# Layer norm without affine parameters: rings of 8-row tiles, statistics combined on GpSimd, a last store in two DMAs

## The chip, the cores and the metric

The kernel runs on one core of a Trainium2 chip. The metric is the device time of one execution in microseconds. Nine runs of the kernel before gave a median of 321.31 us, from 321.01 to 321.41 us. One more execution was recorded by the profiler; all instruction times below are from that one.

## The reference

For each of the 32 x 512 = 16,384 rows of 1024 float32 values the mean and the variance over the row are taken, and the row is normalised with them:

```python
mean = np.mean(x, axis=-1, keepdims=True)
var = np.var(x, axis=-1, keepdims=True)
return ((x - mean) / np.sqrt(var + eps)).astype(np.float32)   # x: (32, 512, 1024), eps = 1e-5
```

67.11 MB are read from HBM and 67.11 MB are written.

## The kernel before

The 16,384 rows are cut into 32 tiles. A tile holds K = 4 rows in each of the 128 partitions, so it is 2 MiB; a partition's four rows lie next to one another in HBM and make one run of 16 KiB. One "row" below always means one row in each of the 128 partitions, 512 KiB in all. So the input has 128 such rows.

For each tile, in the order of the code:

- SyncE (SP) issues the load into `xt` (line 47). The pool `xin` has 6 buffers, 24 rows, so load 7 has to wait until the first tile has been used.
- VectorE (DVE) takes statistics. A `bn_stats` (line 53) covers half a row, 512 values, and leaves six numbers: count, mean and sum of squared deviations, for the even and for the odd values. A `bn_aggr` for each row (line 57) combines the two halves into mean and variance. Then three small instructions on all four rows: the negated mean (line 59), variance plus eps (line 61) and its reciprocal (line 65).
- ScalarE (ACT) takes the square root, which gives `rstd` (line 68), and GpSimd (POOL) multiplies it with the negated mean (line 71).
- ACT normalises row by row (line 75): `Identity` with `scale=rstd` and `bias=nmr`, 128 x 1024 values in each instruction, into `yt`. The pool `yout` has 6 buffers, 24 rows.
- ACT issues the store (line 84).

The order of instructions on each engine is the one that the Tile framework's scheduler chose: the square root of a tile is often put among the normalising instructions of an earlier tile. Loads go through SP's hardware DMA queue (q1 in the profile), stores through ACT's (q10). Both run on the same 16 DMA engines, 8 partitions of a tile on each.

Of the kernel before, what the change touches and what calls it, by code (L numbers as in the profile page):

```python
# [1 line left out]

# [4 lines left out]


@with_exitstack  # L10
def kernel(
    ctx: ExitStack,
    tc: tile.TileContext,
    x: bass.AP,
    eps: bass.AP,
    out: bass.AP,
):
    nc = tc.nc
    P = nc.NUM_PARTITIONS

    eps_val = float(eps) if not isinstance(eps, bass.AP) else 1e-5

    x2 = x.flatten_outer_dims()
    o2 = out.flatten_outer_dims()
    N, D = x2.shape
    BN_MAX = nc.vector.BN_STATS_FMAX
    assert D % BN_MAX == 0
    NSUB = D // BN_MAX

    K = 4  # L30
    rows_per_tile = P * K
    assert N % rows_per_tile == 0
    ntiles = N // rows_per_tile

    xin = ctx.enter_context(tc.tile_pool(name="xin", bufs=6))
    yout = ctx.enter_context(tc.tile_pool(name="yout", bufs=6))
    st = ctx.enter_context(tc.tile_pool(name="st", bufs=4))

    fdt = mybir.dt.float32
    AF = mybir.ActivationFunctionType  # L40
    ALU = mybir.AluOpType

    for t in range(ntiles):
        rows = slice(t * rows_per_tile, (t + 1) * rows_per_tile)

        xt = xin.tile([P, K, D], fdt)
        nc.sync.dma_start(out=xt, in_=x2[rows].rearrange("(p k) d -> p k d", p=P))  # L47

        stats = st.tile([P, K, NSUB, 6], fdt)
        mv = st.tile([P, K, 2], fdt)  # L50
        for k in range(K):
            for s in range(NSUB):
                nc.vector.bn_stats(  # L53
                    out=stats[:, k, s, :],
                    in_=xt[:, k, s * BN_MAX : (s + 1) * BN_MAX],
                )
            nc.vector.bn_aggr(out=mv[:, k, :], in_=stats[:, k, :, :])  # L57
        negmean = st.tile([P, K], fdt)
        nc.vector.tensor_scalar_mul(out=negmean, in0=mv[:, :, 0], scalar1=-1.0)  # L59
        vpe = st.tile([P, K], fdt)  # L60
        nc.vector.tensor_scalar(  # L61
            out=vpe, in0=mv[:, :, 1], scalar1=eps_val, scalar2=None, op0=ALU.add
        )
        ivar = st.tile([P, K], fdt)
        nc.vector.reciprocal(out=ivar, in_=vpe)  # L65

        rstd = st.tile([P, K], fdt)
        nc.scalar.activation(out=rstd, in_=ivar, func=AF.Sqrt, bias=0.0, scale=1.0)  # L68

        nmr = st.tile([P, K], fdt)  # L70
        nc.gpsimd.tensor_mul(out=nmr, in0=negmean, in1=rstd)  # L71

        yt = yout.tile([P, K, D], fdt)
        for k in range(K):
            nc.scalar.activation(  # L75
                out=yt[:, k, :],
                in_=xt[:, k, :],
                func=AF.Identity,
                bias=nmr[:, k : k + 1],
                scale=rstd[:, k : k + 1],  # L80
            )

        dst = o2[rows].rearrange("(p k) d -> p k d", p=P)
        nc.scalar.dma_start(out=dst, in_=yt)  # L84


# [1 line left out]
_INS = ['x', 'eps']  # L88
_OUTS = [((32, 512, 1024), 'float32')]
#: Inputs that are plain numbers.  # L90
_NUMBERS = {'eps': 1e-05}


# [26 lines left out]
```

## Time and profile before

| | us |
|---|---|
| median of nine runs | 321.31 |
| the profiled execution | 320.97 |
| its span, first to last instruction | 318.9 |
| VectorE busy | 181.7 |
| ScalarE busy | 154.2 |
| GpSimd busy | 6.6 |
| normalising, one row (line 75), mean | 1.227 |
| `bn_stats`, half a row (line 53), mean | 0.665 |
| `bn_aggr` (line 57), mean | 0.196 |
| small product on GpSimd (line 71), mean | 0.201 |

The span leaves out 2.07 us of the profiled execution, and that execution is 0.34 us under the median. An instruction's own duration can overlap with the next one's on its engine: in the timeline two `bn_stats` in a row last 1.23 us together, and four normalising instructions 4.63 us. The page adds for the transfers that the 16 DMA engines moved 134.27 MB in the span, and that 6 packets with 0.05 MB came from a queue of kind "instruction": the engines' programs are fetched by the same DMA engines.

### The profile page before, as it was taken

What the parts mean: (1) busy time and instruction counts of PE and PEld (TensorE: products, weight loads), DVE (VectorE), ACT (ScalarE), POOL (GpSimd) and SP (SyncE); (2) the same over time, 40 slices, a digit from 0 to 9 for tenths busy, and PEclk for the clock granted to TensorE, in tenths of its full rate; (3) what the DMA queues carried; (4) which work ended last, traced back from release to release, by engine and by line L of the source; (5) the groups of instructions that cost most, each with busy time, mean ns of one, the idle gap of its engine ahead of it and who ended that gap; (6) DMA issues with size and microseconds to landing.
All of it is one profiled execution on the core that took longest, in us unless ns stands there. A gap on an engine that the chain in (4) does not pass through costs nothing.

```text
span 318.9 us, 926 instructions
## 1 busy us (share of the span) xinstructions
DVE 181.7 (57%) x480; ACT 154.2 (48%) x161; POOL 6.6 (2%) x36
## 2 busy tenths in 40 slices
DVE  0999764457754377544676355765446744467610
ACT  1147491651907419074380833809247091470970
POOL 0000000000000000000000000000000000000000
DMA  7999999999999999999999999999999999999995
GB/s 294 430 411 420 438 434 430 427 429 429 428 434 433 434 430 429 430 430 430 432 438 434 431 430 427 430 430 432 434 434 433 426 432 430 430 427 427 425 427 218
DMA packets 9222, 134.27 MB, mean 421 GB/s; under 512 B 1024, under 2 KB 1024, under 8 KB 1024
## 3 DMA queue, kind: packets, MB, share of 16 engines
q1 hardware_dynamic: 4608, 67.11, 49.6%
q10 hardware_dynamic: 4608, 67.11, 49.2%
q14 instruction: 6, 0.05, 0.0%
HBM read 67.11 MB, written 67.11 MB: 421 GB/s over the span
## 4 chain that ended last, share of the span: by engine, by line
DMA 84%; ACT 4%; issue 4%; DVE 4%; SPq 1%; POOLq 0%; POOL 0%; ACTq 0%; DVEq 0%
DMA xt<-in_x_dram 84%; ACT yt L75 4%; DVE stats L53 3%; SPq L47 1%; DVE mv L57 0%; ACT rstd L68 0%; DVE ivar L65 0%; DVE negmean L59 0%; POOLq L115 0%; POOL nmr L71 0%; DVE vpe L61 0%; ACTq L84 0%; DVEq L65 0%; DVEq L59 0%; ACTq L75 0%
## 5 line engine op out<-in xcount | busy, mean ns | idle before, releaser
L53 DVE BATCH_NORM_STATS2 stats<-xt 128x6 f32<-128x512 f32 x256 | 159.4, 665 | 115.1 <-DMA xt<-in_x_dram 115.1
L75 ACT ACTIVATE yt<-xt,nmr,rstd 128x1024 f32<-128x1024 f32 x128 | 146.7, 1227 | 4.7 <-POOL nmr L71 4.5
L68 ACT ACTIVATE rstd<-ivar 128x4 f32<-128x4 f32 x32 | 6.5, 204 | 149.5 <-DVE ivar L65 149.0
L57 DVE BATCH_NORM_AGGREGATE mv<-stats 128x2 f32<-128x12 f32 x128 | 25.1, 196 | 1.1
L71 POOL TENSOR_TENSOR nmr<-negmean,rstd 128x4 f32<-128x4 f32 x32 | 6.4, 201 | 297.7 <-ACT rstd L68 297.7
L65 DVE RECIPROCAL ivar<-vpe 128x4 f32<-128x4 f32 x32 | 5.7, 178 | 3.0
L59 DVE TENSOR_SCALAR negmean<-mv 128x4 f32<-128x4 f32 x32 | 5.5, 170 | 3.1
L61 DVE TENSOR_SCALAR vpe<-mv 128x4 f32<-128x4 f32 x32 | 5.2, 162 | 0.0
L68 ACT ACT_TABLE_LOAD x1 | 1.3, 1283 | 0.7 <-PEq L101 0.7
L101 POOL MEMSET const-float32-0.0<- 128x1 f32 x1 | 0.1, 99 | 0.2 <-issue 0.2
L101 POOL MEMSET const-bfloat16-1.0<- 128x1 bf16 x1 | 0.1, 102 | 0.0
L101 POOL MEMSET const-uint8-127<- 128x1 uint8 x1 | 0.1, 102 | 0.0
L101 POOL MEMSET const-float32-1.0<- 128x1 f32 x1 | 0.1, 99 | 0.0
## 6 DMA issues: line engine op xcount, KB each, us to landing
xt<-in_x_dram SPq DMA_DIRECT2D x32, 2048.0 KB, 38.4
out_dram<-yt ACTq DMA_DIRECT2D x32, 2048.0 KB, 15.4
```

The lines of the kernel that those rows point to most:

```text
L47: nc.sync.dma_start(out=xt, in_=x2[rows].rearrange("(p k) d -> p k d", p=P))
L53: nc.vector.bn_stats(out=stats[:, k, s, :], in_=xt[:, k, s * BN_MAX : (s + 1) * BN_MAX],)
L57: nc.vector.bn_aggr(out=mv[:, k, :], in_=stats[:, k, :, :])
L59: nc.vector.tensor_scalar_mul(out=negmean, in0=mv[:, :, 0], scalar1=-1.0)
L61: nc.vector.tensor_scalar(out=vpe, in0=mv[:, :, 1], scalar1=eps_val, scalar2=None, op0=ALU.add)
L65: nc.vector.reciprocal(out=ivar, in_=vpe)
L68: nc.scalar.activation(out=rstd, in_=ivar, func=AF.Sqrt, bias=0.0, scale=1.0)
L71: nc.gpsimd.tensor_mul(out=nmr, in0=negmean, in1=rstd)
L75: nc.scalar.activation(out=yt[:, k, :], in_=xt[:, k, :], func=AF.Identity, bias=nmr[:, k : k + 1], scale=rstd[:, k : k + 1],)
L101: nc = _bacc.Bacc("TRN2", target_bir_lowering=False, num_devices=1)
```

## The change

Tiles are 8 rows high (4 MiB, 32 KiB in each partition), 15 of them, and then tiles of 4, 2 and 2 rows. Instead of two pools there are two fixed buffers, used as rings: `xr` for 32 rows of x, and `yr` for 16 rows of y. The framework's scheduler is off (`manual_schedule`): each engine executes in the order of the code.

`bn_aggr` and the small VectorE instructions after it are gone. GpSimd combines the four partial means and four sums of squared deviations of all 8 rows of a tile with nine instructions (the lines of `pool_sum` and `group`), ACT takes the square root of the variance plus eps, VectorE the reciprocal, and GpSimd the product with the negated mean. `std`'s square root now comes before the reciprocal, so VectorE's reciprocal waits for ACT. VectorE goes on to the next tile's `bn_stats` only after it.

The store of the last tile is issued as two DMAs, one for partitions 0 to 119 and one for partitions 120 to 127.

```diff
+TILES = (8, 8, 8, 8, 8, 8, 8, 8, 8, 8, 8, 8, 8, 8, 8, 4, 2, 2)
+XRING = 32
+YRING = 16
+GROUP = 8
+
+def place(tiles, ring):
+    plan, row, pos = [], 0, 0
+    for K in tiles:
+        if pos + K > ring:
+            pos = 0
+        plan.append((K, row, pos))
+        row += K
+        pos += K
+    return plan
...
-    xin = ctx.enter_context(tc.tile_pool(name="xin", bufs=6))
-    yout = ctx.enter_context(tc.tile_pool(name="yout", bufs=6))
+    rings = ctx.enter_context(tc.tile_pool(name="rings", bufs=1))
...
+    xr = rings.tile([P, XRING, D], fdt)
+    yr = rings.tile([P, YRING, D], fdt)
+    eps_t = rings.tile([P, 1], fdt)
...
+    def pool_sum(o, terms):
+        G = terms.shape[1]
+        half = st.tile([P, GROUP, 2], fdt, name="half")
+        nc.gpsimd.tensor_tensor(
+            out=half[:, :G], in0=terms[:, :, 0:2], in1=terms[:, :, 2:4], op=ALU.add
+        )
+        nc.gpsimd.tensor_tensor(
+            out=o, in0=half[:, :G, 0], in1=half[:, :G, 1], op=ALU.add
+        )
...
-            nc.vector.bn_aggr(out=mv[:, k, :], in_=stats[:, k, :, :])
...
+        pool_sum(nmean[:, :G], mean4)
+        nc.gpsimd.tensor_scalar(
+            out=nmean[:, :G], in0=nmean[:, :G], scalar1=-1.0 / H, scalar2=None, op0=ALU.mult
         )
...
+        nc.gpsimd.tensor_mul(out=dev[:, :G], in0=dev[:, :G], in1=dev[:, :G])
+        nc.gpsimd.tensor_scalar(
+            out=dev[:, :G], in0=dev[:, :G], scalar1=float(D // H), scalar2=None, op0=ALU.mult
+        )
+        nc.gpsimd.tensor_tensor(out=dev[:, :G], in0=dev[:, :G], in1=m2, op=ALU.add)
+        pool_sum(ss[:, :G], dev[:, :G])
+        std = st.tile([P, GROUP], fdt, name="std")
+        nc.scalar.activation(
+            out=std[:, :G], in_=ss[:, :G], func=AF.Sqrt, bias=eps_t, scale=1.0 / D
+        )
+        rstd = st.tile([P, GROUP], fdt, name="rstd")
+        nc.vector.reciprocal(out=rstd[:, :G], in_=std[:, :G])
+        nmr = st.tile([P, GROUP], fdt, name="nmr")
+        nc.gpsimd.tensor_mul(out=nmr[:, :G], in0=nmean[:, :G], in1=rstd[:, :G])
...
+    with tc.manual_schedule():
+        nc.vector.memset(eps_t, eps_val)
+        for (K, row, xp), (_, _, yp) in zip(place(TILES, XRING), place(TILES, YRING)):
+            nc.sync.dma_start(out=xr[:, xp : xp + K, :], in_=rows_of(x2, row, K))
+            for g in range(0, K, GROUP):
+                G = min(GROUP, K - g)
+                a, b = xp + g, yp + g
+                group(xr[:, a : a + G, :], yr[:, b : b + G, :], G)
+            dst, src = rows_of(o2, row, K), yr[:, yp : yp + K, :]
+
+            cuts = ((0, 120), (120, P)) if (row + K) * P == N else ((0, P),)
+            for a, b in cuts:
+                nc.scalar.dma_start(out=dst[a:b], in_=src[a:b])
```

More of the change, by code (lines that the diff above doesn't have):

```diff
@@ L26 @@
     BN_MAX = nc.vector.BN_STATS_FMAX
-    assert D % BN_MAX == 0
     NSUB = D // BN_MAX
[L30 to L33, printed above, removed]
-    xin = ctx.enter_context(tc.tile_pool(name="xin", bufs=6))
-    yout = ctx.enter_context(tc.tile_pool(name="yout", bufs=6))
+    assert sum(TILES) * P == N
+    rings = ctx.enter_context(tc.tile_pool(name="rings", bufs=1))
     st = ctx.enter_context(tc.tile_pool(name="st", bufs=4))
@@ L41, with rows_of, group @@
     ALU = mybir.AluOpType
[L43 to L51, printed above, removed]
+    xr = rings.tile([P, XRING, D], fdt)
+    yr = rings.tile([P, YRING, D], fdt)
+    eps_t = rings.tile([P, 1], fdt)
+    def rows_of(a, row, K):
+        return a[row * P : (row + K) * P].rearrange("(p k) d -> p k d", p=P)
+    def pool_sum(o, terms):
[7 more added lines that the diff above has]
+        )
+    def group(xs, ys, G):
+        stats = st.tile([P, GROUP, NSUB, 6], fdt, name="stats")
+        for k in range(G):
             for s in range(NSUB):
@@ L54 @@
                     out=stats[:, k, s, :],
-                    in_=xt[:, k, s * BN_MAX : (s + 1) * BN_MAX],
+                    in_=xs[:, k, s * BN_MAX : (s + 1) * BN_MAX],
                 )
-            nc.vector.bn_aggr(out=mv[:, k, :], in_=stats[:, k, :, :])
[L58 to L62, printed above, removed]
-        )
@@ L64 @@
[L64 to L74, printed above, removed]
+        H = 2 * NSUB
+        parts = stats[:, :G].rearrange("p g s (h c) -> p g (s h) c", h=2)
+        mean4, m2 = parts[:, :, :, 1], parts[:, :, :, 2]
@@ new lines, in group @@
+        nmean = st.tile([P, GROUP], fdt, name="nmean")
+        dev = st.tile([P, GROUP, H], fdt, name="dev")
+        ss = st.tile([P, GROUP], fdt, name="ss")
+        pool_sum(nmean[:, :G], mean4)
+        nc.gpsimd.tensor_scalar(
+            out=nmean[:, :G], in0=nmean[:, :G], scalar1=-1.0 / H, scalar2=None, op0=ALU.mult
+        )
+        nc.gpsimd.tensor_tensor(
+            out=dev[:, :G],
+            in0=mean4,
+            in1=nmean[:, :G].unsqueeze(2).to_broadcast([P, G, H]),
+            op=ALU.add,
+        )
@@ new lines, in group @@
+        nc.gpsimd.tensor_mul(out=dev[:, :G], in0=dev[:, :G], in1=dev[:, :G])
[7 more added lines that the diff above has]
+            out=std[:, :G], in_=ss[:, :G], func=AF.Sqrt, bias=eps_t, scale=1.0 / D
+        )
@@ L75 @@
+        rstd = st.tile([P, GROUP], fdt, name="rstd")
+        nc.vector.reciprocal(out=rstd[:, :G], in_=std[:, :G])
+        nmr = st.tile([P, GROUP], fdt, name="nmr")
+        nc.gpsimd.tensor_mul(out=nmr[:, :G], in0=nmean[:, :G], in1=rstd[:, :G])
+        for k in range(G):
             nc.scalar.activation(
-                out=yt[:, k, :],
-                in_=xt[:, k, :],
+                out=ys[:, k, :],
+                in_=xs[:, k, :],
                 func=AF.Identity,
@@ L81 @@
             )
-        dst = o2[rows].rearrange("(p k) d -> p k d", p=P)
-        nc.scalar.dma_start(out=dst, in_=yt)
+    with tc.manual_schedule():
[10 more added lines that the diff above has]
+                nc.scalar.dma_start(out=dst[a:b], in_=src[a:b])
 _INS = ['x', 'eps']
```

## The prediction, made before the changed kernel was run

> **What bounds the kernel now.** I read the slices of the page first, then the queues, the costliest groups, and the last microseconds by windows.
>
> ```profile
> DMA  7999999999999999999999999999999999999995
> GB/s 294 430 411 420 438 434 430 427 429 429 428 434 433 434 430 429 430 430 430 432 438 434 431 430 427 430 430 432 434 434 433 426 432 430 430 427 427 425 427 218
> ...
> q1 hardware_dynamic: 4608, 67.11, 49.6%
> q10 hardware_dynamic: 4608, 67.11, 49.2%
> q14 instruction: 6, 0.05, 0.0%
> ...
> L53 DVE BATCH_NORM_STATS2 stats<-xt 128x6 f32<-128x512 f32 x256 | 159.4, 665 | 115.1 <-DMA xt<-in_x_dram 115.1
> L75 ACT ACTIVATE yt<-xt,nmr,rstd 128x1024 f32<-128x1024 f32 x128 | 146.7, 1227 | 4.7 <-POOL nmr L71 4.5
> L71 POOL TENSOR_TENSOR nmr<-negmean,rstd 128x4 f32<-128x4 f32 x32 | 6.4, 201 | 297.7 <-ACT rstd L68 297.7
> ```
>
> The DMA engines are full in 38 of 40 slices at about 430 GB/s; VectorE waits 115 us for loads. Only DMA work, and the two ends, can move the time. The end, in windows of one microsecond (columns: window and its length, three engines' busy time, clock, DMA share, GB/s):
>
> ```profile
> 314.00:315.00 1.00, 0.00 (x0) 0.00 (x0) 0.00 (x0) 1.00 0.77 328
> 315.00:316.00 1.00, 0.00 (x0) 0.00 (x0) 0.00 (x0) 1.00 0.16 66
> 316.00:317.00 1.00, 0.00 (x0) 0.00 (x0) 0.00 (x0) 1.00 0.04 16
> 317.00:318.00 1.00, 0.00 (x0) 0.00 (x0) 0.00 (x0) 1.00 0.04 16
> ```
>
> After 316 a single 16 KiB packet is started in each microsecond: one DMA engine of the 16 is late, and the kernel waits for it alone. The trace's packet records say more. Packets of 16 KiB follow each other on an engine every 607 ns; q1 and q10 take turns packet by packet. Most engines finish at 315.2, the late one at 317.75. Following the records back, it is the engine that also fetched instructions at 29.3, 101.3, 179.4 and 248.7 us. The spacing of 70 to 78 us is about 115 VectorE instructions (15 in 9.7 us), so I take these for VectorE's program; the fetches at 83.6 and 239.8, on another engine, for ScalarE's.
>
> It adds up. An engine starts at 1.74, its first packets take some 1.2 us more than later ones, then 512 packets of 607 ns (310.8) and 64 completions of 5 ns (0.3): 314.05. The other engines end at 315.2, so they had 1.15 us of gaps. The late engine had 3.7 us of extra work and ends at 314.05 + 3.7 = 317.75; that is 0.92 us for each of four fetches. The last store lands at 318.0, the span ends at 318.9; 2.07 us lie outside, and the median is 0.34 above this execution.
>
> **What the Trainium skill says.** "DMA: Bandwidth & Descriptors", section "Queues, rings and completion order": a DMA engine takes turns between queues at packet granularity. The trace agrees (q1, q10, q1, ...). The same page, "Why a DMA increments its semaphore by 16 and not by 1": a DMA is spread over the largest k up to 16 that divides its slowest dimension, on the lowest-numbered k engines. So 120 partitions go to 15 engines, 8 on each, and 8 partitions to 8 engines, one on each. No run here shows it yet. "GPSIMD Engine Reference", section 3.1: a two-input GpSimd instruction needs about 2.6 cycles of 1.2 GHz for each element, so an estimated 69 ns for 32 elements against 9 for the 4 of line 71; I add the difference to its 201 ns.
>
> **Part by part.**
>
> *Larger tiles, mid-run.* Each engine moves the same bytes, in 256 packets of 32 KiB in place of 512 (a few smaller at the end). Fetches of 8 KiB took 309 ns and 16 KiB took 611: 302 for each further 8 KiB. So 32 KiB should be pitched at about 1211 ns instead of 1214, 0.7 us less in the run; between 0 and 1.2 us if I vary the fit. Completions fall from 64 to about 37: 0.1 us.
>
> *Do the queues stay full?* One row (512 KiB) takes 1.214 us. Load 0 (8 rows) lands at about 13.4; `bn_stats` 16 x 0.575 = 9.2; nine GpSimd instructions about 2.7 (9 x 0.2, 0.3 for width, 9 waits of 0.05 to 0.08); square root, reciprocal and `nmr` 0.9; eight normalisings 9.3: first store issued at about 35.5, first bytes 36.6. By then (36.6 - 2.9) / 1.214 = 27.8 rows are read. The x ring holds 32, and its first slot came free at 35.5, so reads never stop. From here a tile of loads and one of stores share 19.4 us. The compute loop on VectorE and GpSimd takes 9.2 + 2.7 + 0.6 = 12.5, ScalarE 10: hidden. The y ring has two tiles: ScalarE waits for the store two tiles back, normalises in 9.3 and issues while the other store has 9 us to go: hidden too. The 25.1 us of `bn_aggr` and 16.4 of small VectorE instructions that go away, and the 180 on GpSimd that come, are therefore worth nothing in mid-run.
>
> *The end.* Reads lead by 27.8 rows, so when row 120 is read (36.6 + 92 x 2.428 = 260.0) 92 are stored. Now load packets are smaller than the 32 KiB store packets but still alternate with them: 4 rows read for 8 stored until 274.6, then 2 for 8 twice: 286.7 and 298.8. 12 rows of stores are left, to 313.3. The last tile: landing 0.4, `bn_stats` 2.3, GpSimd 2.4, the three small steps 0.9, two normalisings 2.3, issue to first byte 1.0 (load 0: 0.74 to 1.74): 308.1. The stores ahead of it end at 310.9, so the chain has 2.8 us of cover; uncovered it would cost its excess one for one. The y ring's waits for tiles 13 to 15: 11 us against stores that last 12 to 14.6 while loads are mixed in. So most of the 1.15 us of gaps goes too, but only on engines that weren't last.
>
> *The late engine.* VectorE has 276 instructions instead of 480 (the reciprocal is the one left beside `bn_stats`). The first fetch came after some 45, the next after 115 more each. I expect two in place of four, 1.85 us saved. GpSimd's 187 may fetch once on an engine of its own, harmless. If a fetch delays by one packet slot and the slot is now 32 KiB, a fetch costs 1.5 and the saving falls to 0.7.
>
> *Two stores at the end.* The sixteenth engine is spared 8 packets of 8 KiB, 2.4 us; engines 0 to 7 get one more, 0.3 us; the second issue (0.34) is covered by the first one's 2.4 us of data. It pays only if the late engine is the sixteenth. In the order in which the engines' first packets start, the late one is eighth, with three engines out of order; so I lean to "not the sixteenth", and take +0.3.
>
> *Sum,* last packet of the late engine: 314.05 - 0.7 - 0.1 + 2 x 0.92 + 0.3 = 315.4 against 317.75: **-2.4 us**. Median 321.31 - 2.4 = 318.9; I say **318.8**.
>
> **Rivals.**
>
> 1. *The split meets the late engine.* Then its 1.85 us are outweighed by the 2.4 spared, and the others decide: 314.05 - 0.8 + 0.3 + 0.4 of gaps = 313.95, -3.8 us: 317.5. For: two stores of this form make sense only so. Against: the start order.
> 2. *Nothing gained.* The late engine keeps 3.7 us of delay (dearer or more fetches) and 32 KiB packets cost twice 607: 314.05 - 0.1 + 3.7 + 0.3 = 317.95: 321.5, within the noise of before. For: the fetch counts are inferred.
> 3. *Slower: stores start late and the y ring stalls.* In the trace the first store was issued at 19.59 and its first packet started at 23.44, 3.8 us later instead of 1.0. In the last 40 us a y slot's loop is then 9.3 + 3.8 + 0.4 + 0.3 = 13.8 us against stores of 12.1 with 2-row loads beside them, and against 9.7 with none: 1.7 to 4.1 us of empty queue for each of one or two tiles, some 3.9 in all: 318.8 + 3.9 = 322.7. It decides from a start delay of about 2.1 (12.1 - 9.3 - 0.7), and makes the kernel slower from about 3.2. Against: the last store of before, issued at 309.25, followed its predecessor at 310.3 without a gap. A GpSimd chain of over 7.8 us would do the same; 0.2 us an instruction speaks against it.
>
> **How the numbers follow.** Forecast 0.48, rival 1 0.28, rival 2 0.12 (half of it still faster), rival 3 0.12. Faster by over 0.2% (0.64 us, about what a measurement of this kernel can tell from no change): 0.48 + 0.28 + 0.06 = 0.82; same 0.06; slower 0.12. The range goes from rival 1 with 0.6 us more off the packets, 316.9, to 320.9, which takes in the dearer fetch (320.0) and half of rival 2; the slower case is left out.
>
> **What would show it.** Right: GB/s at 430 or a little more until the last slices; q1 and q10 at about half their packets; the last microseconds with one engine at work for about 1.5 us instead of 2.5; `yr` waiting for its store some 9 us a tile without DMA slices falling; last store issued near 308. The split's worth shows as a DMA share that falls at once (rival 1) or trails (forecast). Wrong: slices below 9 after 270 us (rival 3), GpSimd instructions well over 0.3 us, more instruction fetches than four, or packets of 32 KiB that take over 1.22 us.

## The result

The changed kernel takes 318.8 us, the median of nine runs (318.64 to 319.32), against 321.29 us for the kernel before (28 runs). The ratio is 0.9926, with a 95% interval from 0.9918 to 0.9934: 2.5 us or 0.8% faster. The profiled execution's span fell from 318.9 to 316.8 us.

The page of the changed kernel, in the lines that answer those of before:

```profile
span 316.8 us, 750 instructions
...
DMA  8999999999999999999999999999999999999996
GB/s 331 418 443 422 434 398 418 447 434 426 456 405 451 410 455 407 455 414 451 426 439 447 414 447 411 455 405 459 410 455 422 439 443 432 426 440 424 417 419 248
...
q1 hardware_dynamic: 2592, 67.11, 49.6%
q10 hardware_dynamic: 2599, 67.11, 49.4%
q14 instruction: 5, 0.04, 0.0%
...
L113 ACT ACTIVATE yr<-xr,nmr,rstd 128x1024 f32<-128x1024 f32 x128 | 146.7, 1227 | 117.5 <-DMA out_dram<-yr 115.4
L77 DVE BATCH_NORM_STATS2 stats<-xr 128x6 f32<-128x512 f32 x256 | 153.4, 676 | 12.3 <-DMA xr<-in_x_dram 12.3
```

The DMA engines are still full from end to end. What changed is who waits. Before, VectorE waited 115 us for loads; now ScalarE waits 115.4 us for stores to leave the y ring, and VectorE waits for a load only once, at the start. Neither costs anything while the DMA line stays at 9. GB/s swings from slice to slice (405, 455) because the page counts a packet, now 32 KiB, whole in the slice in which it starts.

The end, in windows of one microsecond (window, length, three engines' busy time, clock, DMA share, GB/s):

```profile
311.00:312.00 1.00, 0.00 (x0) 0.00 (x0) 0.00 (x0) 1.00 1.02 336
312.00:313.00 1.00, 0.00 (x0) 0.00 (x0) 0.00 (x0) 1.00 0.91 279
313.00:314.00 1.00, 0.00 (x0) 0.00 (x0) 0.00 (x0) 1.00 0.84 287
314.00:315.00 1.00, 0.00 (x0) 0.00 (x0) 0.00 (x0) 1.00 0.48 156
315.00:316.00 1.00, 0.00 (x0) 0.00 (x0) 0.00 (x0) 1.00 0.04 16
```

The tail with a single engine at work is gone: the last packet ends at 315.4 instead of 317.75. But the last store is slow. For three microseconds the engines are nearly as busy as ever, and move 280 to 340 GB/s instead of 430: by the packet records its 8 KiB packets take 0.40 us in the mean, where 0.31 is usual in this trace.

So the total was met. Whether it was met for the reasons given had to be tested, because three terms of different sign made it up.

### The profile page after: what moved, and what is told of

Read it like the earlier page. It is cut to its first block, busy times and chain, and to the rows that moved or that the text cites. A ratio compares the mean times of both kernels' runs of the same rounds, so it can differ in the third digit from the quotient of the medians.

```text
span 316.8 us, 750 instructions
## 1 busy us (share of the span) xinstructions
DVE 155.6 (49%) x275; ACT 153.4 (48%) x147; POOL 41.6 (13%) x184
## 3 DMA queue, kind: packets, MB, share of 16 engines
q1 hardware_dynamic: 2592, 67.11, 49.6%
q10 hardware_dynamic: 2599, 67.11, 49.4%
## 4 chain that ended last, share of the span: by engine, by line
DMA 64%; ACT 23%; DVE 7%; POOL 2%; issue 1%; ACTq 0%; POOLq 0%
DMA out_dram<-yr 60%; ACT yr L113 22%; DVE stats L77 7%; DMA xr<-in_x_dram 4%; POOL half L66 0%; ACT std L105 0%; POOL dev L99 0%; POOL dev L102 0%; POOL dev L92 0%; POOL nmean L89 0%; POOL dev L98 0%; POOL nmean L69 0%; POOL ss L69 0%; DVE rstd L109 0%; ACTq L133 0%
## 5 line engine op out<-in xcount | busy, mean ns | idle before, releaser
L113 ACT ACTIVATE yr<-xr,nmr,rstd 128x1024 f32<-128x1024 f32 x128 | 146.7, 1227 | 117.5 <-DMA out_dram<-yr 115.4
L77 DVE BATCH_NORM_STATS2 stats<-xr 128x6 f32<-128x512 f32 x256 | 153.4, 676 | 12.3 <-DMA xr<-in_x_dram 12.3
L66 POOL TENSOR_TENSOR half<-stats 128x16 f32<-128x16 f32 (+2 forms) x18 | 4.2, 232 | 161.3 <-DVE stats L77 161.3
L105 ACT ACTIVATE std<-ss,eps_t 128x8 f32<-128x8 f32 (+2 forms) x18 | 5.4, 300 | 37.6 <-POOL ss L69 31.5
L99 POOL TENSOR_SCALAR dev<-dev 128x32 f32<-128x32 f32 (+2 forms) x18 | 5.2, 291 | 1.6
L102 POOL TENSOR_TENSOR dev<-dev,stats 128x32 f32<-128x32 f32 (+2 forms) x18 | 4.5, 251 | 1.5
L92 POOL TENSOR_TENSOR dev<-stats,nmean 128x32 f32<-128x32 f32 (+2 forms) x18 | 4.3, 239 | 1.5
L98 POOL TENSOR_TENSOR dev<-dev 128x32 f32<-128x32 f32 (+2 forms) x18 | 4.2, 234 | 1.4
L89 POOL TENSOR_SCALAR nmean<-nmean 128x8 f32<-128x8 f32 (+2 forms) x18 | 4.2, 231 | 1.6
L66 POOL TENSOR_TENSOR half<-dev 128x16 f32<-128x16 f32 (+2 forms) x18 | 3.9, 215 | 1.4
```

The lines of the kernel that those rows point to most:

```text
L66: nc.gpsimd.tensor_tensor(out=half[:, :G], in0=terms[:, :, 0:2], in1=terms[:, :, 2:4], op=ALU.add)
L77: nc.vector.bn_stats(out=stats[:, k, s, :], in_=xs[:, k, s * BN_MAX : (s + 1) * BN_MAX],)
L89: nc.gpsimd.tensor_scalar(out=nmean[:, :G], in0=nmean[:, :G], scalar1=-1.0 / H, scalar2=None, op0=ALU.mult)
L92: nc.gpsimd.tensor_tensor(out=dev[:, :G], in0=mean4, in1=nmean[:, :G].unsqueeze(2).to_broadcast([P, G, H]), op=ALU.add,)
L98: nc.gpsimd.tensor_mul(out=dev[:, :G], in0=dev[:, :G], in1=dev[:, :G])
L99: nc.gpsimd.tensor_scalar(out=dev[:, :G], in0=dev[:, :G], scalar1=float(D // H), scalar2=None, op0=ALU.mult)
```

## The experiments

Three terms had to be told apart: fewer fetches of VectorE's program, larger packets, and the split of the last store. The main rival: the gain is the larger tiles' alone.

**The changed kernel again,** as the measure for the three runs beside it on the same chip: one store, more VectorE instructions, and tiles of 4 rows.

> The changed kernel once more, beside the others on one chip. All theories: ratio to the kernel before 0.992 to 0.9935 (318.8 us), span about 316.8. The theory on record (fewer instruction fetches of VectorE, about 1.85 us, and packets of 32 KiB, about 0.7 us) says that the DMA engines again end between 313.5 and 315.4, the last of them one that fetched instructions twice.

319.0 us, ratio 0.9933 [0.9921, 0.9945]. The packet records put the engines' ends between 313.7 and 315.7 us, except for one that ends at 311.1; the last is 0.3 later than expected.

**The last store in one DMA.**

```diff
-            cuts = ((0, 120), (120, P)) if (row + K) * P == N else ((0, P),)
+            cuts = ((0, P),)
```

> The changed kernel with the last store in one DMA of 128 partitions. Theory 1 (the split doesn't meet the late engine and costs: it gives engines 0 to 7 a packet more, and the 120-partition DMA over 15 engines moved its 8 KiB packets at 280 GB/s in 311 to 314 us): the last store runs at 430 GB/s again, the last packet ends near 314.9 instead of 315.4, median 0.3 to 0.6 us below that of the changed kernel. Rival (the split relieves the engine that ends last): median 0.5 to 2.4 us above it. Second rival (it doesn't matter): within 0.2 us.

318.47 us, ratio 0.9924 [0.9908, 0.994], 0.53 below the changed kernel beside it, though the intervals of the two overlap. The same windows:

```profile
311.00:312.00 1.00, 0.00 (x0) 0.00 (x0) 0.00 (x0) 1.00 1.03 434
312.00:313.00 1.00, 0.00 (x0) 0.00 (x0) 0.00 (x0) 1.00 1.00 426
313.00:314.00 1.00, 0.00 (x0) 0.00 (x0) 0.00 (x0) 1.00 0.59 246
314.00:315.00 1.00, 0.00 (x0) 0.00 (x0) 0.00 (x0) 1.00 0.08 33
```

The store runs at full speed, most engines end at 313.6, and one ends at 315.1, alone again. In the changed kernel the engine that the split spares was done at 311.1, before all others: the late engine is another one. Rival 1 of the prediction falls.

**More VectorE instructions that nobody waits for.**

```diff
+            if K == 8:
+                for j in range(16):
+                    nc.vector.memset(idle[:, j : j + 1], 0.0)
```

> The changed kernel with 16 memsets of 128x1 on VectorE after each of the fifteen 8-row tiles: 240 instructions that nobody waits for, VectorE busy some 14 us more in time that it spends waiting, 516 instructions in all. Theory 1 (VectorE's instruction fetches make one DMA engine late): two more fetches on the same engine, the late engine's last packet 1.4 to 2 us later, time 1.4 to 2 us above the changed kernel. Rival (the gain came from packet size and the end alone): within 0.2 us of the changed kernel.

320.41 us, 1.4 above the changed kernel, at the lower edge of what the theory expects and far from the rival's 0.2. In the page, VectorE's 240 instructions and the fetches are what changed:

```profile
DVE 160.6 (50%) x515; ACT 153.4 (48%) x147; POOL 41.2 (13%) x184
...
q14 instruction: 7, 0.06, 0.0%
```

Two fetches more, 7 instead of 5. Before the last store the latest engine is 2.2 us behind the median engine (314.0 against 311.8), compared with 1.5 in the changed kernel beside it. The memsets don't hold up the end by themselves: the last store is issued at 310.40, while the median engine is busy with the store before it until 311.8.

**Fewer VectorE instructions in the kernel before.**

```diff
-            nc.vector.bn_aggr(out=mv[:, k, :], in_=stats[:, k, :, :])
...
-        nc.vector.tensor_scalar_mul(out=negmean, in0=mv[:, :, 0], scalar1=-1.0)
+        nc.vector.tensor_scalar_mul(out=negmean, in0=stats[:, :, 0, 1], scalar1=-1.0)
...
-            out=vpe, in0=mv[:, :, 1], scalar1=eps_val, scalar2=None, op0=ALU.add
+            out=vpe, in0=stats[:, :, 0, 2], scalar1=eps_val, scalar2=None, op0=ALU.add
```

> The kernel before without its 128 bn_aggr on VectorE: mean and variance are read from the first half-row's numbers, so the output is not the reference's; loads, stores, buffers and packets are as before, VectorE has 352 instructions instead of 480. Theory 1 (the kernel before ends with the DMA engine that fetches VectorE's instructions, 0.92 us a fetch): one or two fetches fewer, 0.7 to 1.9 us faster than the kernel before, 319.3 to 320.5. Rival (VectorE's instructions don't matter, the larger packets and the end do): 321.0 to 321.4.

320.46 us, ratio 0.9977 [0.997, 0.9983]: 0.77 us faster.

```profile
DVE 164.9 (52%) x352; ACT 154.3 (48%) x161; POOL 6.5 (2%) x36
...
q14 instruction: 5, 0.04, 0.0%
```

There are 5 fetches instead of 6. VectorE's 25 us of `bn_aggr` can't explain the gain by themselves, since VectorE waited for loads in both. Nor do the ends: the first store's first packet starts at 23.4 us in both, and in the kernel before the last store followed its predecessor without a gap. Together the two runs price a fetch at 0.7 to 0.8 us: one fetch fewer here, 1.4 for two more above.

The packet records show the delay itself. They don't name the DMA engine, but on one engine each packet starts some 4 ns before the last one ends, and every engine gets 8 packets of each 128-partition DMA; so they can be strung together. VectorE's fetches then lie on one engine in each of four runs. A fetch holds the engine for 0.31 us, and the packet right behind it takes longer than its kind:

| kernel | VectorE's fetches at, us | the packet behind each, us | usual | fetches and delays in all, us |
|---|---|---|---|---|
| before | 29.3, 101.3, 179.4, 248.7 | 1.144, 1.222, 0.953, 1.232 | 0.611 | 3.3 |
| before, without `bn_aggr` | 42.4, 140.5, 238.6 | 1.136, 1.135, 1.207 | 0.611 | 2.6 |
| changed | 44.5, 191.6 | 1.568, 1.832 | 1.213 | 1.6 |
| changed, with memsets | 31.5, 95.8, 171.7, 250.1 | 1.826, 1.751, 1.852, 1.809 | 1.213 | 3.6 |

So one of VectorE's fetches costs its DMA engine 0.65 to 0.95 us. In the kernel before and in the changed kernel, no packet between 45 and 300 us is over 0.2 us longer than its kind, except behind a fetch. The difference of 0.8 between the first two rows is what the run gained. Between the last two rows it is 2.0, and the time rose by 1.4; where the rest went isn't traced. Why the packet behind a fetch takes longer isn't shown either. And one thing doesn't follow from the simple picture: without `bn_aggr` the late engine still ends 2.6 us after the median engine, as before, and both end some 0.45 us earlier. That the others wait for the late engine's loads during the run would fit; it wasn't tested.

**16 KiB packets in the same tiles.** Each of the first 12 tiles is laid over HBM as two blocks of 4 rows in each partition; the tile's side of each DMA is cut in two in the same way (left out below).

```diff
+        if row < 96:
+            return a[row * P : (row + K) * P].rearrange("(h p k) d -> p h k d", h=2, p=P)
...
```

> The changed kernel, tiles, order, rings, semaphores and instructions as they are, but each of the first 12 tiles (96 of 128 rows) is laid over HBM as two blocks of 4 rows for each partition, so that loads and stores consist of packets of 16 KiB; the last 32 rows keep 32 KiB. Theory 1 (a packet costs some 5 ns beside its bytes: 607 against 1209 ns in the two traces): 192 packets more on each engine, 192 x 4.5 = 0.9 us above the changed kernel (0.5 to 1.1). Rival (packet size is worth nothing): within 0.2 us.

322.96 us, ratio 1.0055 [1.0042, 1.0068]: 4 us above the changed kernel, where 0.9 was expected. Both theories missed it, and the windows say where most of it went (a long one in mid-run, then two at the end):

```profile
60.00:260.00 200.00, 93.87 (x166) 94.57 (x90) 23.21 (x100) 1.00 1.01 432
...
280.00:290.00 10.00, 5.42 (x11) 9.02 (x10) 2.32 (x10) 1.00 0.86 370
290.00:300.00 10.00, 4.53 (x9) 9.06 (x9) 2.14 (x10) 1.00 0.86 367
```

The DMA engines have 14% of gaps between 280 and 300, some 2.8 us. The edit changes packets in the first 12 tiles only. So from 200 us on loads come in 32 KiB packets, while the stores beside them, of earlier tiles, have 16 KiB until 275 us. Taking turns by packet, loads get two thirds: from 200 to 220 us they moved 5.8 MB and stores 3.1. The last load packet ends at 278 us instead of 295.5, stores are left alone, and the y ring's loop (normalise 9.2, start the store, land it) is longer than a store of 9.7 us without company. This is the y-ring stall of rival 3, from another cause; that the larger packets brought it about is read from this one trace. The mid-run, still without gaps, is the usable part of this run. The same window in the kernel before and in the changed kernel:

```profile
60.00:260.00 200.00, 114.48 (x302) 99.66 (x105) 4.02 (x20) 1.00 1.01 431
```

```profile
60.00:260.00 200.00, 98.37 (x173) 99.85 (x95) 25.53 (x109) 1.00 1.00 434
```

431, 432 and 434 GB/s. By the packet records, between 50 and 200 us, before the loads here change to 32 KiB, 64.62 MB of data went through before, 64.68 here, 64.92 in the changed kernel. The other traces of the changed kernel's tiles lie within 0.03 of that. The packets' share is 0.24 of 64.92, 0.37%, or an estimated 1.2 us over some 310; packets and all else in mid-run 0.30 of 64.92, 1.45 us.

**Tiles of 4 rows.**

```diff
-TILES = (8, 8, 8, 8, 8, 8, 8, 8, 8, 8, 8, 8, 8, 8, 8, 4, 2, 2)
+TILES = (4,) * 31 + (2, 2)
```

> The changed kernel with 31 tiles of 4 rows and two of 2, all else as it is: packets of 16 KiB, GpSimd 330 instructions, VectorE 290. Theory 1 (32 KiB packets are worth 0.7 us through a pitch of 1211 instead of 1214 ns, and the fetches matter): 0.4 to 1.2 us above the changed kernel, still 1.3 to 2.1 below the kernel before. Rival (larger tiles carry the gain): as slow as the kernel before. Second rival (tile height is worth nothing): within 0.2 us of the changed kernel.

325.73 us, ratio 1.0144 [1.0131, 1.0157]: slower than the kernel before, as none of the theories had it. The waits of this run (engine and line, for whom, us in total, times, longest) and its timeline:

```profile
ACT std L105 <- POOL ss L69: 97.6, 30, 13.7
...
ACT std L105 <- DMA xr<-in_x_dram: 41.2, 3, 23.8
```

```profile
253.68 0.34 ACTq L133 DMA_DIRECT2D out_dram<-yr  x1
254.06 0.30 ACT L105 ACTIVATE std<-ss,eps_t 128x4 f32<-128x4 f32 x1 [23.79 <-DMA xr<-in_x_dram]
```

ScalarE, which only has to issue a store that is ready, stands for 23.8 us until a load lands. The trace shows which one: loads and stores alike report their landing on eight semaphores, handed out in turn. The store that goes out at 253.68 uses the semaphore of the load issued at 217.23, which landed at 253.60. With eight loads of 4 rows in a 32-row ring, and stores beside them, eight don't suffice. The changed kernel, with four loads of 8 rows and at most two stores, has no such wait. After the stall each 4-row tile takes 8.0 us on the way from VectorE over GpSimd and ScalarE back to VectorE, against 4.86 for its store. So the lost lead is never made up, and the slices from 300 us on fall to about 300 GB/s.

**Tiles of 4 rows with a ring for four loads.**

```diff
-XRING = 32
+XRING = 16
```

> Tiles of 4 rows as in the run before with 31 of them, but with an x ring of 16 rows, so that only four loads are outstanding. Theory A (that run lost its 6.7 us because ScalarE's store had to wait 23.8 us at 230 to 253 us for a load: eight semaphores are shared by the outstanding loads and stores, and with eight loads in flight a store got one that a load still held): no such wait, 0.5 to 2 us above the changed kernel. Rival B (tiles of 4 rows are slow at the end because VectorE, GpSimd and ScalarE need 8.0 us for each, against 4.86 us of store, whatever the semaphores do): as slow as that run, 5 us or more above the changed kernel.

No verdict: the four runs lay between 322.84 and 336.73 us, a spread that no other kernel here has. In the profiled execution, of 329.43, ScalarE no longer stands for a load, but even the fastest run is 4 us above the changed kernel. So the semaphores are not the whole of it. How much is the 8.0 us chain's stays open, and how much the smaller x ring's, which this edit brings with it.

**Three tiles in each ring.**

```diff
-XRING = 32
-YRING = 16
+XRING = 24
+YRING = 24
```

> The changed kernel with both rings of 24 rows (3 tiles each) instead of 32 and 16. Theory 1 (the y ring's wait of some 9 us a tile is hidden, and what the x ring has to cover is the start: the first slot comes free at 35.6 us, three loads are read by 1.7 + 1.2 + 24 x 1.214 = 32 us, so the load queue stands empty until 36.6 us, and nothing that is lost there comes back): 4 to 6 us slower than the changed kernel, the DMA share low between 32 and 37 us. Rival (the y ring of two tiles costs something that a third tile gives back): faster than the changed kernel, by up to 1 us. Second rival (the DMA engines find other work): within 0.3 us.

328.64 us, ratio 1.0231 [1.0217, 1.0245], 9.8 above the changed kernel. The expected hole is there, and a second one at the end:

```profile
30.00:35.00 5.00, 5.00 (x10) 5.00 (x5) 0.00 (x0) 1.00 0.24 105
35.00:40.00 5.00, 1.76 (x5) 1.57 (x3) 2.34 (x10) 1.00 0.73 216
...
310.00:320.00 10.00, 2.64 (x5) 2.67 (x3) 2.06 (x10) 1.00 0.68 288
```

Missing shares of 3.8 and 1.35 us up to 40, 5.1 in all. At the end 3.2 us more are missing between 310 and 320, which I had not counted. Reads lead stores by at most 24 rows here instead of 27.8, so fewer stores are left to cover the last tiles' chain; that this is the cause is argued, not tried. What a third y tile would gain beside a full x ring this run can't tell, as it changes both rings.

**The split once more, and another cut.** The changed kernel, one store, and the cut at partition 112, side by side on one chip.

> The changed kernel a third time, as the measure for the next two on this chip: 318.6 to 319.1 us.

> The changed kernel with one last store, a second time. If the 0.53 us of the first pair is the split's cost, 0.3 to 0.7 us below the changed kernel of this call, the last packet near 315.1, and the last three microseconds of stores at 420 to 435 GB/s. If it was chance, within 0.2 us.

```diff
-            cuts = ((0, 120), (120, P)) if (row + K) * P == N else ((0, P),)
+            cuts = ((0, 112), (112, P)) if (row + K) * P == N else ((0, P),)
```

> The changed kernel with the last store cut at partition 112 instead of 120: 7 partitions on each of 16 engines and then one on each of 16. Theory A (what costs is that the 120 partitions are dealt out over 15 engines, 8 neighbours to each): the 112 are dealt out unevenly too, 7 neighbours to each, so the last store is slow again, 250 to 350 GB/s, and the time is that of the changed kernel or up to 0.3 us less, as no engine gets a ninth packet. Theory B (what costs is the second DMA and its packet on engines 0 to 7): full speed and as fast as with one store.

318.8, 318.42 and 318.29 us; ratios 0.9932 [0.992, 0.9945], 0.991 [0.9895, 0.9925] and 0.9913 [0.9899, 0.9926]. One store is again about 0.4 us ahead of the changed kernel, and the two intervals still overlap a little. Taken together, the two pairs have 10 runs with the split and 10 without; the one without is faster in 81 of the 100 ways to pair them. In the profiled execution with one store, a late one of 319.24, the store ran at 434 GB/s as expected, but the last packet ended at 316.0 instead of 315.1. The cut at 112 is as fast as one store. Its windows:

```profile
311.00:312.00 1.00, 0.00 (x0) 0.00 (x0) 0.00 (x0) 1.00 1.03 393
312.00:313.00 1.00, 0.00 (x0) 0.00 (x0) 0.00 (x0) 1.00 1.05 377
```

A slightly slower store, not one at 280: its 8 KiB packets take 0.35 us in the mean, against 0.31 with one store and 0.40 to 0.43 in three traces of the cut at 120. Theory A falls on the numbers it gave. Theory B has its time right and the full speed not quite, and a second DMA alone costs nothing. Two things differ between the cuts: at 120 the data are on 15 engines and move slowly, and eight engines get a ninth packet. No run separates the two, and why those packets take longer stays open.

**Fewer, longer VectorE instructions** in the version with one store.

```diff
-    NSUB = D // BN_MAX
+    NSUB = 1
...
+        nc.vector.tensor_reduce(
+            out=rest[:, :G], in_=xs[:, :, BN_MAX:], op=ALU.add, axis=mybir.AxisListType.X
+        )
...
```

With half the partial sums, GpSimd's two `pool_sum` calls need one instruction each instead of two (left out above).

> The changed kernel with one last store and fewer, longer VectorE instructions: only the first half of each row goes through bn_stats, the other half of a whole tile through one tensor_reduce whose result nobody uses, so that VectorE is busy for about as long but has 165 instructions instead of 275. Mean and variance come from half a row, so the output is not the reference's. Theory 1 (each fetch of VectorE's program makes one DMA engine 0.9 us later, and that engine ends last): one fetch instead of two, the last engine's packet 0.7 to 1.1 us earlier than with one store alone, 317.3 to 317.8 us. Rival (the last engine is late for another reason): 318.2 to 318.6, as with one store alone.

318.19 us, ratio 0.9907 [0.989, 0.9924]. That is the rival's number.

```profile
DVE 148.6 (47%) x165; ACT 153.4 (48%) x147; POOL 31.3 (10%) x148
...
q14 instruction: 4, 0.03, 0.0%
```

A fetch has gone, but not one of VectorE's. Whose program a fetch brings can be told from how many instructions, as the page counts them, each engine had begun by then. In the changed kernel the fetch at 123.3 us comes at ScalarE's 52nd instruction. With rings of 24 rows it comes at 115.6, again at ScalarE's 52nd, while VectorE and GpSimd stand elsewhere than before: it is ScalarE's. The fetches at 86.8 and 302.8 come at GpSimd's 53rd and 174th instruction, with 24-row rings at its 54th and 174th, and lie on one DMA engine: they are GpSimd's.

In this run the edit cuts GpSimd to 148 instructions, and its second fetch is the one that has gone; its first and ScalarE's come together at 123 us. VectorE still has two, at its 54th and 164th of 165 instructions (93.1 and 304.6 us). They lie on one DMA engine, and that engine ends last, at 315.0, as VectorE's did with one store (315.1). The edit missed its aim: it left VectorE with two fetches, and the unchanged end is what the fetch theory says for two. So this run doesn't test the theory.

## Why the prediction was right, point by point

*What bounds the kernel* held: every slice but the first and last is full in both kernels.

*The late engine* (1.85 us from two fetches fewer): right in kind. The changed kernel has VectorE's fetches at 44.5 and 191.6 us, two as counted. GpSimd has two, not the one that was allowed for, and ScalarE one. The size was a little off: the runs price a fetch at 0.7 to 0.8 us, not 0.92, which makes this term 1.4 to 1.6 us; the packet records make it 3.3 - 1.6, some 1.75. The 0.92 came from taking all that was left of the late engine's time for the fetches' own; the records give the four 0.83 in the mean. The cause is shown from both sides, with instructions added to the changed kernel and taken from the one before, and by the delays in the records. What the prediction did not see is how near the next engine is: with one store, the one with GpSimd's two fetches ends at 314.4, 0.7 us before VectorE's. By that trace, more fetches saved on VectorE could gain an estimated 0.7 us and no more.

*Packets* (0.7, and 0.1 for completions): too small. A 32 KiB packet takes 1213 ns in the records, two of 16 KiB take 2 x 611, with an overlap of 4 ns for each packet in both: 5 ns saved for each pair instead of the 3 that I worked out from fetches of 8 KiB. The mid-run gives 1.2 us for packet size and 1.45 with everything else that it holds, both estimates.

*The split* (+0.3, on the wrong engine): right in sign, and the two pairs of runs say 0.4 to 0.5. The slow last store was not foreseen; how much of the cost is its, and how much the ninth packet's 0.3 us, is open. The Trainium skill's rule for the number of engines ("DMA: Bandwidth & Descriptors", section "Why a DMA increments its semaphore by 16 and not by 1") is confirmed: q10 has 2599 packets with the split and 2592 with one store, which is 15 + 8 completions in place of 16. So the 8 partitions do go to eight engines; which eight, the records don't show.

With the measured terms: 1.4 to 1.75 and 1.45, less 0.4 to 0.5, make 2.35 to 2.8; measured 2.5. The mechanism was right, but that the total came out within 0.1 us was partly luck: packets were worth 0.65 us more than predicted, while fetches were worth 0.1 to 0.45 less and the split cost 0.1 to 0.2 more.

*Do the queues stay full?* The steps land where the working put them: first `bn_stats` at 13.11 (13.4 predicted), GpSimd's nine instructions in 2.8 us (2.7), first store issued at 35.64 (35.5). Its first packet came only at 39.8 instead of 36.6, a start delay of 4 us like that of the first store before; the load queue covered it, as loads were still waiting there. ScalarE's wait for the y ring is 8.2 us a tile (about 9). The x ring's four tiles are needed, as the 24-row run shows.

*The end* was hidden, but by less than stated, and this is the step of the working that was wrong. I followed the last tile from its own landing to a store at 307.1. Its timeline says otherwise:

```profile
295.64 4.63 ACT L113 ACTIVATE yr<-xr,nmr,rstd 128x1024 f32<-128x1024 f32 x4 [2.54 <-DMA out_dram<-yr]
...
300.69 0.30 ACT L105 ACTIVATE std<-ss,eps_t 128x2 f32<-128x2 f32 x1 [0.42 <-ACT yr L113]
301.02 0.17 DVE L109 RECIPROCAL rstd<-std 128x2 f32<-128x2 f32 x1 [5.31 <-ACT std L105]
301.12 2.47 DVE L77 BATCH_NORM_STATS2 stats<-xr 128x6 f32<-128x512 f32 x4
...
309.44 0.93 ACTq L133 DMA_DIRECT2D out_dram<-yr  x2
```

The 4-row tile waits for the y ring until 295.64. The next tile's square root stands behind its normalising, VectorE's reciprocal behind that square root, and the last tile's `bn_stats` behind the reciprocal, though its load had landed by 295.5. The last store is issued at 309.44 and could start at about 310.4. The store before it ends at 311.07 on the median engine. Cover: an estimated 0.6 us, not 2.8.

*Rival 2* (nothing gained) falls with the result. *Rival 3* (y-ring stalls) did not occur: no slice after 270 us fell, but the last. Its mechanism is real all the same, as the run with mixed packet sizes shows. In the changed kernel loads never have larger packets than the stores beside them.

**A faster version** came out of it: the changed kernel with one last store, 318.42 and 318.47 us, or with the cut at 112, 318.29. Both beat the kernel before clearly; against the changed kernel the gain of 0.4 to 0.5 us is near what these runs can resolve.

## What to carry to other kernels

When every DMA slice is full, look at the last microseconds one by one: if a single engine is still at work, ask what it did that the others did not. Here it fetched programs, and each of VectorE's fetches cost the kernel 0.7 to 0.8 us, so the number of instructions on an engine that waits half of the time had a price. In these runs queues that took turns by packet shared the engines in the ratio of their packet sizes, so the sizes at the end are worth choosing so that loads don't outrun stores. And before an experiment removes a fetch, find out whose it is.

## What the runs showed that was not expected

- The packet right behind a program fetch is itself longer, by 0.34 to 0.64 us behind VectorE's fetches, on top of the fetch's 0.31.
- A store can wait for an unrelated load: 23.8 us on ScalarE in the run with 31 tiles of 4 rows, where eight loads in flight and the stores shared eight semaphores.
- A 120-partition store over 15 engines took 0.40 to 0.43 us for each 8 KiB packet in the mean of three traces, the same rows over 16 engines 0.31.
- Loads of 32 KiB beside stores of 16 KiB opened 2.8 us of gaps at the end of a kernel whose mid-run did not change.
